# Where ninety products of an output projection stand beside a recurrence: one constant in a hybrid recurrent block

## The chip, the cores and the metric

The kernel runs on one core of one Trainium2 chip. The metric is the device time of one execution in microseconds (us), as the median of several runs. The engines are named as in the profile: PE (TensorE, with its weight loads PEld), DVE (VectorE), ACT (ScalarE), POOL (GpSimd) and SP (SyncE, which issues the transfers).

## What is computed

One layer of a diffusion backbone on 1024 latent tokens and a prefix of 256 context tokens, D = 1024, all in float32. Two token mixers read the same modulated input: an RG-LRU (width 1280, a linear recurrence over tokens in two directions) and an RWKV-7 (16 heads of 64, a matrix recurrence in two directions). Their outputs are merged and a SwiGLU follows.

```python
def wkv7_scan(r, w, k, v, a, b, S0):          # the second recurrence
    def step(S, inp):
        sa = jnp.einsum('dbhij,dbhj->dbhi', S, a_t)
        S = S * w_t[..., None, :] + sa[..., :, None] * b_t[..., None, :] + v_t[..., :, None] * k_t[..., None, :]
        y = jnp.einsum('dbhij,dbhj->dbhi', S, r_t)

def merge(lru, rwkv, g_lru, g_rwkv, p):
    m = sigmoid(g_lru) * (lru @ p['w_o_lru']) + sigmoid(g_rwkv) * (rwkv @ p['w_o_rwkv'])
    return m @ p['w_out']

x = x + g_m * merge(...)
x = x + g_f * swiglu(modulate(rms_norm(x)), w_ffn_in, w_ffn_out)
```

The change concerns `lru @ w_o_lru` (1024 tokens, 1280 inputs, 1024 outputs), "the products" below, and the steps of `wkv7_scan` beside which they run.

## The kernel before

A float32 product is made from three TensorE products of parts: each operand is split into a high part (`hi`) and a rest (`lo`), and hi·hi, hi·lo and lo·hi are accumulated. A 128x512 output tile of `lru @ w_o_lru` needs 10 blocks of inputs times 3, so 30 products; there are 2 halves of the tokens (q) times 8 blocks of outputs (o), 16 tiles, 480 products in all.

The program is written as phases. Input projection, the RG-LRU and the preparation of the RWKV operands come first. `phase_b` runs the RWKV recurrence in 40 steps of 32 tokens: steps 0 to 7 are the context, steps 8 to 39 the latents. The heads are in two halves a = 0, 1, each a generator (`wkv_chain`). One step of one half is, on PE, `ru<-tvu,skb` (16 products into PSUM tile `ru`), then a copy to `rs`, then `ru<-rs,xc` (16 products), four copies of 32 rows from `ru` into the state tile `tvu`, then `pn<-tvu,ska` and two copies into the next `tvu`, and for latent steps `py<-tvu,skb`, which gives the output rows `y`. The copies alternate between ACT and DVE (`copy`, L990). So a half is a chain PE, ACT or DVE, PE, ACT or DVE, PE; the other half and the products fill what lies between. Names carry the step and the half: `ru8_0` is step 8, half 0.

The products come from the generator `lru_out` (L1058 to L1098). For q it first makes ten split inputs: loads `lh` and `lu`, a GELU on `lu` (ACT), `lh*lu` (POOL), the high part `lhi` (ACT, L68) and the rest `llo` (POOL, L69); ten buffers each. Then for each o it loads `olr` (640 KB, a single buffer), makes `olh` (ACT, L68, two casts) and `oll` (POOL, L69, two subtractions), two buffers each, loads `olg` and takes its sigmoid (ACT), issues 30 products into PSUM tile `pol` (two buffers, L1092), multiplies on DVE (L1097) and stores `t1`. The tile of q = 0, o = 4 is `pol0_4`. The generator hands out one product at each call.

`phase_b` calls it in two ways. `FILL0` products are drawn before `wkv_setup`; the others are drawn inside the loop over steps, at two places of each step, in a count that grows with the step so that `480 - FILL0 - TAIL` are out at the end; `TAIL` (45) are left behind the loop. While a product is drawn inside the loop, `k.pe_after` ties it behind the last scan product on PE by an ordering edge.

What order the engines get is not the order of the code. The framework records all instructions with a priority (their place in the code) and then lists them, engine by engine, by simulating the program with a model of durations; buffers of a pool and the ordering edges limit it. Each engine executes its list in that order. So drawing a product earlier in the code gives it a better priority and fewer ties; where it ends up on each engine is decided by that listing.

Of the kernel before, what the change touches and what calls it, by code (L numbers as in the profile page):

```python
# [1097 lines left out]
            nc.sync.dma_start(k.t1_d[o * P:(o + 1) * P, sl], g)  # L1098


FILL0 = 0
LASTN = 2
CTXP = 8
CTXO = 0
# [18 lines left out]
def phase_b(k):  # L1123
    tc = k.tc
    k.gnp = k.root.enter_context(tc.tile_pool(name="gnp", bufs=1, side="right"))
    with tc.tile_pool(name="bp", bufs=1) as k.bp, tc.tile_pool(name="olp", bufs=1) as op, \
# [6 lines left out]
        done = 0  # L1133
        for _ in range(FILL0):
            next(fill)
# [6 lines left out]
        for s in range(NSTEP + 1):  # L1142
            for i, a in enumerate((0, 0, 1, 0, 1, 1, 0, 1)):
# [15 lines left out]
                if i in FILLAT:  # L1159
                    at = s + (FILLAT.index(i) + 1) / len(FILLAT)  # L1160
                    while done < (480 - FILL0 - TAIL) * (at + CTXW * min(at, 8)) / (NFEND + 8 * CTXW):
                        next(fill, None)
# [523 lines left out]
```

## Time and profile before

| | us |
|---|---|
| runs | 3083.84, 3095.47, 3108.86 (median 3095.47) |
| the profiled execution | 3079.55, span 3077.7 |
| PE busy | 2707.6 (88%) |
| DVE, ACT, POOL busy | 1890.6, 1456.4, 1012.4 |
| mean granted TensorE clock | 0.924 |
| the scan's latent steps, from the trace | about 1684 to 2093 |

The profiled execution lies 15.9 us under the median of the runs. Busy time is a union of the records of an engine; the profile cuts the span into 40 slices of 77 us each for the curves of busy tenths and granted clock.

### The profile page before, as it was taken

The page shows a single profiled execution, that of the slowest core. Times are in us where ns is not written, and L with a number is a line of the kernel's source. Part 1 is how long each engine was busy: PE and PEld are TensorE (multiplying, and loading weights), DVE is VectorE, ACT ScalarE, POOL GpSimd, SP SyncE. Part 2 cuts the span into 40 slices and gives each one's busy share as a digit, 9 for nine tenths or more (in the row PEclk, how much of TensorE's full clock was granted, in tenths as well). Part 3 has the DMA queues.
Part 4 walks back from the last instruction along what each step waited for, and adds up shares of the span by engine and source line. Part 5 has one row for each costly group of instructions (what it writes and reads, how often), then busy time and mean ns, then how long its engine had stood idle before and what let it go on. Part 6 is the DMA issues. An engine that isn't in the chain of part 4 may idle for free. (4 is left out here: it accounts for less than half of the span.)

```text
span 3077.7 us, 57133 instructions
## 1 busy us (share of the span) xinstructions
PE 2707.6 (88%) x22526; PEld 2159.6 (70%) x22526; DVE 1890.6 (61%) x2843; ACT 1456.4 (47%) x2647; POOL 1012.4 (33%) x896
## 2 busy tenths in 40 slices
PE   5988988889899878887889788777999999999998
PEld 4776766667677666676656666555788888888888
DVE  7588898994667977889872333564785323223234
ACT  3476777783467565767433343454334111111114
POOL 4344444452445555666333130235431000000000
PEclk9899999999999979988569998888999999999999
DMA  5333334322455456556766787988753111121112
GB/s 207 95 117 123 124 104 134 111 85 77 133 152 146 119 123 141 124 137 158 200 196 218 228 258 220 253 252 261 269 214 127 58 48 50 41 61 42 42 57 73
DMA packets 379602, 429.18 MB, mean 139 GB/s; under 512 B 134166, under 2 KB 286150, under 8 KB 371398
## 3 DMA queue, kind: packets, MB, share of 16 engines
q1 hardware_dynamic: 379334, 425.53, 47.4%
q8 instruction: 178, 2.92, 0.4%
q14 instruction: 90, 0.74, 0.1%
HBM read 286.87 MB, written 126.26 MB: 134 GB/s over the span
## 5 line engine op out<-in xcount | busy, mean ns | idle before, releaser
L88 PE MATMUL pin<-h1024hi,whi 128*128 128x512 f32 (+1 forms) x1024 | 430.5, 421 | 47.5 <-DVE whi L230 15.4
L90 PE MATMUL pin<-h1024hi,wlo 128*128 128x512 f32 (+1 forms) x1024 | 420.9, 414 | 10.7 <-POOL wlo L231 10.6
L89 PE MATMUL pin<-h1024lo,whi 128*128 128x512 f32 (+1 forms) x1024 | 425.8, 416 | 4.1 <-DVE h1024lo L120 4.1
L231 POOL TENSOR_TENSOR wlo<-wraw,whi 128x512 fp32r<-128x512 f32 (+1 forms) x144 | 211.7, 1471 | 306.6 <-DVE whi L230 167.8
L88 PEld LDWEIGHTS pin<-h1024hi,whi 128*128 128x128 f32 (+1 forms) x1024 | 203.3, 199 | 102.0 <-DVE whi L230 15.9
L90 PEld LDWEIGHTS pin<-h1024hi,wlo 128*128 128x128 f32 (+1 forms) x1024 | 201.5, 197 | 64.5 <-POOL wlo L231 17.7
L89 PEld LDWEIGHTS pin<-h1024lo,whi 128*128 128x128 f32 (+1 forms) x1024 | 203.4, 199 | 50.0 <-DVE h1024lo L120 6.6
L54 ACT ACT_TABLE_LOAD x164 | 210.4, 1283 | 18.3 <-DVE gd L499 5.9
L987 PE MATMUL pn<-tvu,ska 128*64 128x64 f32 (+1 forms) x2496 | 157.4, 250 | 36.1 <-ACT tvu L990 19.2
L1434 DVE TENSOR_TENSOR sil<-sil,pfu 128x512 f32<-128x512 f32 x44 | 30.3, 688 | 242.0 <-PE pfu L90 242.0
L388 DVE SCALAR_TENSOR_TENSOR lxc<-lup,c_lru_conv_w,lxc 120x512 f32<-120x512 f32 (+3 forms) x198 | 161.1, 837 | 15.9 <-ACT lxc L386 15.2
L987 PEld LDWEIGHTS pn<-tvu,ska 128*64 128x64 f32 (+1 forms) x2496 | 119.9, 156 | 71.8 <-ACT tvu L990 23.8
L1442 DVE SCALAR_TENSOR_TENSOR x<-pfo,modv,x 128x512 f32<-128x512 f32 (+1 forms) x112 | 74.2, 671 | 132.4 <-PE pfo L90 132.4
L990 ACT COPY tvu<-ru 32x256 f32<-32x256 f32 x193 | 70.1, 363 | 126.8 <-DVE tvu L990 77.8
L68 ACT CAST whi_fi<-wraw_fi 128x1024 fp32r<-128x1024 f32 x48 | 50.5, 1053 | 167.6 <-PE pfg L89 50.4
L724 DVE TENSOR_TENSOR it<-bp,X 128x62 f32<-128x62 f32 (+25 forms) x186 | 122.1, 657 | 3.9
L230 DVE CAST whi<-wraw 128x512 fp32r<-128x512 f32 (+1 forms) x144 | 76.3, 531 | 76.3 <-PE pin L89 36.6
L687 ACT COPY bc<-pm 32x256 f32<-32x256 f32 x160 | 98.8, 617 | 50.9 <-PE pm L683 48.4
L673 PE MATMUL pkt<-c_ident,kb 128*128 128x128 f32 x320 | 59.2, 315 | 65.6 <-DVE kb L657 41.5
L987 PE MATMUL ru<-tvu,skb 128*32 128x64 f32 (+1 forms) x2560 | 93.0, 243 | 26.8 <-ACT tvu L990 8.7
L725 DVE TENSOR_TENSOR X<-X,it 128x62 f32<-128x62 f32 (+25 forms) x186 | 113.7, 611 | 3.9
L432 POOL TENSOR_TENSOR lxc<-la 120x512 f32<-120x512 f32 (+3 forms) x66 | 86.8, 1318 | 80.1 <-ACT la L54 68.3
(374 smaller groups left out, 7512.9 us busy)
## 6 DMA issues: line engine op xcount, KB each, us to landing
skb<-skb_d SPq DMA_DIRECT2D x40, 1024.0 KB
wraw<-in_w_in_dram SPq DMA_DIRECT2D x142, 256.0 KB
wraw_fi<-in_w_ffn_in_dram SPq DMA_DIRECT2D x48, 512.0 KB
skb_d<-kr SPq DMA_DIRECT2D x160, 128.0 KB
ska_d<-kt SPq DMA_DIRECT2D x160, 128.0 KB
skb_d<-km SPq DMA_DIRECT2D x160, 128.0 KB
ska<-ska_d SPq DMA_DIRECT2D x40, 512.0 KB
wmr<-in_w_modT_dram SPq DMA_DIRECT2D x32, 512.0 KB
```

Source lines behind the costliest of these rows:

```text
L54: ins = self.nc.scalar.activation(*a, **b).ins
L88: nc.tensor.matmul(out, wh, xh, start=first, stop=False)
L89: nc.tensor.matmul(out, wh, xl, start=False, stop=False)
L90: nc.tensor.matmul(out, wl, xh, start=False, stop=last)
L230: nc.vector.tensor_copy(hi, raw)
L231: (nc.gpsimd if INLO else nc.vector).tensor_tensor(lo, raw, hi.bitcast(F32), ALU.subtract)
L388: nc.vector.scalar_tensor_tensor(xc, tap(j), k.lcw[r, t, d, j:j + 1], xc, ALU.mult, ALU.add)
L432: nc.gpsimd.tensor_tensor(xc, a, a, ALU.mult)
L687: nc.scalar.copy(bc[g, :, 4 * i:4 * i + 4].rearrange("s t e h -> s h e t"), pm[64 * c + 32:64 * c + 64, :, d, :, 32:64])
L724: nc.vector.tensor_tensor(tv, bpt[:, :, t + 1:32, t:t + 1].to_broadcast(sh), X[:, :, t:t + 1, 0:t + 1].to_broadcast(sh), ALU.mult)
L725: nc.vector.tensor_tensor(X[:, :, t + 1:32, 0:t + 1], X[:, :, t + 1:32, 0:t + 1], tv, ALU.add)
L987: k.pe_last = nc.tensor.matmul(*a, **b, start=True, stop=True).ins.name
```

## The change

One constant. `FILL0` is the number of products that are drawn from `lru_out` before the set-up of the scan, without a tie to a scan product; with 90 of them drawn there, the loop draws 345 instead of 435 over the same steps.

```diff
-FILL0 = 0
+FILL0 = 90
```

The code that reads it:

```python
        for _ in range(FILL0):
            next(fill)
        with tc.high_priority(offset=SETO):
            wkv_setup(k)
...
                    while done < (480 - FILL0 - TAIL) * (at + CTXW * min(at, 8)) / (NFEND + 8 * CTXW):
                        next(fill, None)
                        done += 1
```

What this does to the engines' lists is seen at three places. First PE, around the last products of `ru8_0` that read the first latent block `xc8` (step 8, half 0). Before:

```order
L1092 MATMUL pol0_4_16072<-lhi0_8_15083,olh0_4_16063 128x512
L987 MATMUL pn7_1_16238<-tvu1_1_14937,ska1_14925 64x64 x16
L987 MATMUL ru8_0_16218<-rs8_0_16235,xc8_15994 32x64 x10
L1092 MATMUL pol0_4_16072<-llo0_8_15084,olh0_4_16063 128x512
L1092 MATMUL pol0_4_16072<-lhi0_8_15083,oll0_4_16064 128x512
L1092 MATMUL pol0_4_16072<-lhi0_9_15093,olh0_4_16063 128x512
L1092 MATMUL pol0_4_16072<-llo0_9_15094,olh0_4_16063 128x512
L1092 MATMUL pol0_4_16072<-lhi0_9_15093,oll0_4_16064 128x512
L987 MATMUL ru8_1_16285<-tvu1_2_14938,skb2_14929 32x64 x2
```

And of the change, at the same scan products:

```order
L1092 MATMUL pol0_5_15813<-llo0_9_15021,olh0_5_15804 128x512
L1092 MATMUL pol0_5_15813<-lhi0_9_15020,oll0_5_15805 128x512
L987 MATMUL ru8_0_16306<-rs8_0_16323,xc8_16102 32x64 x12
L1092 MATMUL pol0_6_16097<-lhi0_0_14930,olh0_6_16088 128x512
L1092 MATMUL pol0_6_16097<-llo0_0_14931,olh0_6_16088 128x512
L987 MATMUL ru8_0_16306<-rs8_0_16323,xc8_16102 32x64
L987 MATMUL ru8_1_16372<-tvu1_2_15168,skb2_15159 32x64 x13
L1092 MATMUL pol0_6_16097<-lhi0_0_14930,oll0_6_16089 128x512
L1092 MATMUL pol0_6_16097<-lhi0_1_14940,olh0_6_16088 128x512
```

The tile `pol0_5` stands wholly ahead of the end of `ru8_0` and most of `pol0_6` ahead of `pn8_0`; before, both are spread over steps 8 to 15. Counted over the whole list, the products ahead of the first scan product of a step are 90 and 90 (before, and of the change) at step 7, 92 and 107 at step 8, 155 and 213 at step 9, 256 and 295 at step 19, 328 and 353 at step 28, 419 and 419 at step 38.

Second, PE in one round of a later step (step 20, half 0), before:

```order
L987 MATMUL ru20_0_18391<-rs20_0_18408,xc20_18153 32x64 x16
L1092 MATMUL pol1_0_18130<-lhi1_4_18065,oll1_0_18122 128x512
L1092 MATMUL pol1_0_18130<-lhi1_5_18075,olh1_0_18121 128x512
L1092 MATMUL pol1_0_18130<-llo1_5_18076,olh1_0_18121 128x512
L1092 MATMUL pol1_0_18130<-lhi1_5_18075,oll1_0_18122 128x512
L1092 MATMUL pol1_0_18130<-lhi1_6_18085,olh1_0_18121 128x512
L987 MATMUL py19_1_18476<-tvu1_1_14937,skb1_14928 32x64 x12
L987 MATMUL ru20_1_18500<-tvu1_2_14938,skb2_14929 32x64 x16
```

And of the change:

```order
L987 MATMUL ru20_0_18443<-rs20_0_18460,xc20_18207 32x64 x16
L1092 MATMUL pol1_1_18012<-llo1_7_17204,olh1_1_18003 128x512
L1092 MATMUL pol1_1_18012<-lhi1_7_17203,oll1_1_18004 128x512
L1092 MATMUL pol1_1_18012<-lhi1_8_17213,olh1_1_18003 128x512
L987 MATMUL py19_1_18526<-tvu1_1_15167,skb1_15158 32x64 x16
L987 MATMUL ru20_1_18550<-tvu1_2_15168,skb2_15159 32x64 x16
```

A round holds four or five products before and three or four with the change.

Third, ACT in step 8: `olh0_5`, `olh0_6` and so on are the casts of the projection's weights, `olg` its gates, `lu1`, `lhi1` the inputs of the second half of the tokens, and the L990 rows the copies of the scan. Before:

```order
L68 CAST olh0_5_16347<-olr0_5_16345 128x640 x2
L54 ACTIVATE olg0_5_16353<-olg0_5_16353 128x512
L990 COPY tvu0_2_14935<-ru8_0_16218 32x256 x3
L990 COPY tvu0_0_14933<-pn8_0_16304 64x512
L990 COPY tvu1_2_14938<-ru8_1_16285 32x256 x2
L68 CAST olh0_6_16879<-olr0_6_16877 128x640 x2
L990 COPY tvu1_2_14938<-ru8_1_16285 32x256
L990 COPY ys8_0_16398<-py8_0_16381 128x256
```

And of the change:

```order
L68 CAST olh0_5_15804<-olr0_5_15802 128x640 x2
L54 ACTIVATE olg0_5_15810<-olg0_5_15810 128x512
L68 CAST olh0_6_16088<-olr0_6_16086 128x640 x2
L54 ACTIVATE olg0_6_16094<-olg0_6_16094 128x512
L990 COPY tvu0_2_15165<-ru8_0_16306 32x256 x3
L68 CAST olh0_7_16435<-olr0_7_16433 128x640 x2
L54 ACTIVATE olg0_7_16441<-olg0_7_16441 128x512
L54 ACT_TABLE_LOAD
L54 ACTIVATE lu1_0_17128<-lu1_0_17128 128x512
L54 ACTIVATE lu1_1_17138<-lu1_1_17138 128x512
L990 COPY tvu0_0_15163<-pn8_0_16391 64x512
L990 COPY tvu1_2_15168<-ru8_1_16372 32x256 x2
```

The casts of `olh0_6` and `olh0_7`, the table load and the first two GELUs of the second half stand ahead of the copy from `pn8_0`; before, `olh0_7` and the GELUs stand in steps 11 and 12. A few rows further down in the list of the change, the cast of `olh1_0` and one more GELU stand ahead of the copy from `pn8_1`; before, it stands in step 14.

## Rows read from the trace of the kernel before

**Rows 1.** The profile's page: the span, and PE's busy tenths and granted clock in 40 slices
```profile
span 3077.7 us, 57133 instructions
...
PE   5988988889899878887889788777999999999998
...
PEclk9899999999999979988569998888999999999999
```
**Rows 2.** Busy time of each engine by stretch, then granted clock, DMA share, GB/s
```profile
core 0: us, PE busy (x) PEld busy (x) DVE busy (x) ACT busy (x) POOL busy (x), PEclk, DMA share, GB/s
1620.00:1684.00 64.00, 61.08 (x809) 43.50 (x811) 16.39 (x30) 20.14 (x41) 25.01 (x15) 0.97 0.73 231
1684.00:1912.00 228.00, 185.46 (x4995) 142.75 (x4990) 78.12 (x150) 88.99 (x200) 43.47 (x32) 0.92 0.80 234
1912.00:2093.00 181.00, 137.38 (x3111) 103.61 (x3099) 103.66 (x141) 86.05 (x225) 62.89 (x28) 0.86 0.84 241
2093.00:2170.00 77.00, 63.46 (x349) 48.00 (x350) 38.95 (x49) 38.48 (x79) 36.09 (x15) 0.84 0.87 271
```
**Rows 3.** PE in order of time, end of step 7 and step 8: start, us, instruction
```profile
1668.82 0.39 PE L1092 MATMUL pol<-lhi,olh 128*128 128x512 f32 x1
1669.05 0.40 PE L1092 MATMUL pol<-llo,olh 128*128 128x512 f32 x1
...
1671.81 0.39 PE L1092 MATMUL pol<-llo,olh 128*128 128x512 f32 x1
1672.13 0.31 PE L987 MATMUL ru<-rs,xc 32*32 32x64 f32 x8
...
1678.32 0.33 PE L987 MATMUL pn<-tvu,ska 128*64 128x64 f32 x2
```
**Rows 4.** The tile xc, issues of its loads: duration ns, first and last start
```profile
L975 SPq DMA_DIRECT2D xc<-x_d x8: 320/400/1146, 1624.6 to 1972.9; - x8
```
**Rows 5.** ACT in order of time, steps 7 to 9; in brackets idle before and releaser
```profile
1651.47 1.35 ACT L68 CAST olh<-olr 128x640 fp32r<-128x640 f32 x2 [1.12 <-DMA olr<-in_w_o_lru_dram]
...
1665.89 1.35 ACT L68 CAST olh<-olr 128x640 fp32r<-128x640 f32 x2 [9.80 <-DMA olr<-in_w_o_lru_dram]
...
1675.42 1.36 ACT L68 CAST olh<-olr 128x640 fp32r<-128x640 f32 x2 [5.30 <-DMA olr<-in_w_o_lru_dram]
...
1680.37 0.58 ACT L990 COPY tvu<-pn 64x512 f32<-64x512 f32 x1 [1.44 <-PE pn L987]
1681.22 0.75 ACT L990 COPY tvu<-ru 32x256 f32<-32x256 f32 x2 [0.27 <-PE ru L987]
1683.74 1.35 ACT L68 CAST olh<-olr 128x640 fp32r<-128x640 f32 x2 [1.77 <-DMA olr<-in_w_o_lru_dram]
...
1688.06 0.56 ACT L990 COPY tvu<-pn 64x512 f32<-64x512 f32 x1
```
**Rows 6.** ACT, then PE, in order of time at steps 12 and 13
```profile
1724.99 0.63 ACT L54 ACTIVATE olg<-olg 128x512 f32<-128x512 f32 x1 [5.01 <-DMA olg<-gl_d]
1725.62 1.28 ACT L54 ACT_TABLE_LOAD   x1
1726.92 1.15 ACT L54 ACTIVATE lu<-lu 128x512 f32<-128x512 f32 x2
...
1728.51 1.12 PE L987 MATMUL pn<-tvu,ska 128*64 128x64 f32 x16 [5.67 <-ACT tvu L990]
...
1732.93 0.63 PE L1092 MATMUL pol<-llo,olh 128*128 128x512 f32 x1
1733.35 0.63 PE L1092 MATMUL pol<-lhi,oll 128*128 128x512 f32 x1
```
**Rows 7.** What PE waited for, 1684 to 2093: total us, times, longest
```profile
PE pn L987 <- ACT tvu L990: 16.9, 10, 5.7
PE ru L987 <- issue: 16.7, 12, 2.4
PE py L987 <- issue: 14.5, 8, 3.7
```

## The prediction

> **What bounds the kernel now.** I read the page first, then the busy time by stretch, then PE and ACT in order of time. On the page PE is the busiest engine and its granted clock is ragged in the middle of the span [rows 1]. The change touches the scan there, so the stretches count. From 1620 to 1684 us (the end of the context steps and latent step 8) PE is busy for 61.1 of 64 us at a granted clock of 0.97: PE itself is the bound, and the products that stand between the scan's matmuls delay the scan one for one. From 1684 to 2093 (steps 9 to 39) PE is busy for 185.5 of 228 and 137.4 of 181 us, at 0.92 and 0.86 [rows 2]: 86 us of PE are idle, and a step is a chain PE, copy, PE, copy. After 2093 come the 45 products of the tail, behind the scan in PE's list, and the merge, which needs the last outputs of the scan, so I let a delay of the scan's end reach the end of the kernel in full.
>
> Two things are to be seen in the rows. Products follow each other on PE at 0.23 us at full clock (1668.82 to 1669.05 [rows 3]) and at 0.42 us at half clock (1732.93 to 1733.35 [rows 6]). And the first matmuls of step 8 that need `xc8` run at 1672.13 (some just before) [rows 3], although that load was issued at 1624.6 [rows 4], more than 40 us earlier. So PE does not wait for it. The simulated listing must see a long wait there, since it packs products in front of these matmuls; on the chip there is none.
>
> **The change part by part.** First, the ninety products themselves: in both lists 90 stand ahead of step 7, nearly the same ones at the same places. Taking the tie away moves nothing there: 0 us. No instruction is added or removed; every load, cast and store of the projection exists as before.
>
> Second, step 8. Ahead of step 9 stand 213 products instead of 155: 58 more. PE has 2.9 us idle in that stretch [rows 2], so they are paid: 58 x 0.23 = 13.3 us. The lower bound would be 0 if the wait for `xc8` were real; the rows say it is not, so I take 13.3.
>
> Third, their weights. ACT executes in order, and the casts of `olh` wait for loads. A load into the single buffer `olr` starts when POOL has finished with the tile before; the casts run at 1651.47, 1665.89, 1675.42 and 1683.74, each after an idle wait for the load [rows 5], that is rounds of 14.4, 9.5 and 8.3 us. With the change the casts of `olh0_6` and `olh0_7`, a gate (0.63), a table load (1.28) and two GELUs (1.15) stand ahead of the copy from `pn8_0`. Two rounds after 1675.42 at 8.3 to 9.5 us are 1692.1 to 1694.5; with the cast (1.36) and the rest this is 1696.5 to 1698.9 for a copy that ran at 1680.37 [rows 5, 6]: 16.1 to 18.5 us late, 2.8 to 5.2 us more than the products alone make it. I take 4.0. Behind that copy stands `pn8_0`'s successor `ru9_0` on PE, and then the whole chain. The cast of `olh1_0` one round later, ahead of the copy from `pn8_1` (1688.06 [rows 5]), gives about the same. SP's queue moves too: the loads of `olr` and the stores of `t1` come earlier between the same scan loads, and the DMA engines are busy for 0.73 of the stretch, less than later [rows 2]; I put 0 on it.
>
> Fourth, a stall that goes. At step 12 ACT waits 5.01 us for the gate's load, then does the table load and the two GELUs, and PE stands idle for 5.67 us behind it [rows 6]. That group now lies in step 8 and is in the third term: -5.7 us. If something else takes its place there, 0.
>
> Fifth, what steps 9 to 38 get back. They lose the 58 products, 33 before step 28 and 25 after. At the granted clocks of 0.92 and 0.86 a share of 16% and 28% of the time is at half clock, so a product is worth 0.26 and 0.28 us: 33 x 0.26 + 25 x 0.28 = 15.6 us if PE were the bound in every round. If every round ended on a copy or another wait, it would be 0. There are 60 rounds (30 steps, two halves), each one product shorter, and the three largest causes alone make 30 waits of PE in them [rows 7]. A round that already waits only waits longer. So I take half: -7.8 us.
>
> Sum: 13.3 + 4.0 - 5.7 - 7.8 = +3.8 us. On the profiled execution's 3079.55 this is 3083.4; that execution lies 15.9 us under the median of the runs, and the prediction is for a median: 3095.47 + 3.8, or 3099.
>
> **The rivals.** *The scan thins out and the clock falls.* In the rows the granted clock falls with PE's density: 0.97 at 95% busy, 0.92 at 81%, 0.86 at 76% [rows 2]. The change takes about one product in five out of every round. If the stretch at 0.92 falls to 0.86 and the one at 0.86 to 0.80, the share at half clock grows by 12% of the time, 27 + 22 = 49 us; PE is busy for 79% of it and does half the work, so 49 x 0.79 / 2 = 19 us are lost: 3.8 + 19 = +23, or 3118. Against it: PE loses about 0.5 us of work (two products) in a step of 13.6 (409 us over 30 steps). The Trainium skill, "TensorE: Matmul & The Clock Gate", section "HAM oscillation — how this bites in real kernels", says that gaps in matmul work bring the half clock back, again and again in a loop with waits. The trace agrees so far as its ragged clock goes; by that rule the change would cost these 23 us instead of 4.
>
> *The free gap.* The step 8 wait is real, or PE reaches it with time to spare, and the 58 products fill it: 0 + 4.0 - 5.7 - 7.8 = -9.5, or with everything given back -17: 3078 to 3086. For it speaks only that the listing put them there; against it the load of `xc8` [rows 4] and the full PE [rows 2].
>
> *ACT's queue is the bound in step 8 (the slower side).* Place: the casts of `olh0_6`, `olh0_7` and `olh1_0` ahead of the scan's copies. If each round of load, cast and subtraction takes the 14.4 us that one of them took [rows 5], the third comes at 1718.6, the copy from `pn8_1` at 1721 instead of 1688.06: 33 us late, 19.6 beyond the products, so +19.4 in all: 3115. It is slower by over 1% (31 us) from rounds of about 18 us. For it: all four casts of [rows 5] waited for their load, and the copies of the ten inputs of the second half also move from steps 12 to 17 up into steps 8 to 12. Against it: the two rounds at that very place took 9.5 and 8.3.
>
> **How the numbers follow.** The forecast with its own range, from all given back and no ACT term (13.3 - 5.7 - 15.6 = -8) to nothing given back and the upper ACT term (13.3 + 5.2 - 5.7 = +13), is 3087 to 3108: chance 0.56. The clock 0.15, the free gap 0.12, ACT's queue 0.13, anything else 0.04. The runs of the kernel before lie 11.6 us under and 13.4 us over their median, and a median of new runs can lie several us off as well. So the range is 3082 to 3125: it takes in the clock and ACT's queue at their prices and most of the free gap. About 1% (31 us) is what a measurement of this kernel can tell from no change. Faster by that needs the free gap, all given back and more: 0.03. Slower by that needs the clock or ACT's queue at more than the prices above, or both: 0.12. Within 1%: 0.85.
>
> **What would show it.** Right: PE stays above 90% busy through step 8, the first `ru<-rs,xc` of step 9 comes 13 to 19 us later than before against the end of step 7, ACT's row `olh<-olr` waits for the load two or three times in that stretch with an L990 copy directly behind, no idle PE of 5 us at step 12, and steps 9 to 38 shorter by about 14 us in sum (a quarter us each, and the stall). Wrong, second step: step 9 begins no later. Wrong, third: the copy from `pn8_0` runs right behind its matmuls. Wrong, fifth: steps 9 to 38 as long as before (then +11), with PE waiting more on copies; or longer, with a granted clock under 0.90 from 1700 on, which is the clock's case. If the mean clock and the length of the context steps change, the first step was wrong.

## The result, and the profile after

The change makes the kernel slower: 3105.76 us (3098.09 to 3114.50) beside 3083.85 us (3073.88 to 3108.86) for the kernel before on the same chip, a ratio of 1.0067 (95% interval 1.0055 to 1.0079), so +20.7 us by the ratio. A second measurement gave 1.0081 (1.0061 to 1.0100). That is within 1%, and 3105.76 lies in the range, but the forecast was a step of +3.8 us, so about 17 us were not foreseen. The rest of this text looks for them.

From the page of the change, the lines that answer to [rows 1]: span, and PE's busy tenths and granted clock in 40 slices.
```profile
span 3099.1 us, 57147 instructions
...
PE   5888888889899878896889888678899999999998
...
PEclk9999999899999879997568898868999999999999
```
Busy time of each engine by stretch (columns as in [rows 2]), cut at the same work as there: up to the end of step 7 and most of step 8, the rest of step 8, steps 9 to 28, 28 to 39.
```profile
1620.00:1684.00 64.00, 62.37 (x553) 42.77 (x552) 11.99 (x21) 17.37 (x34) 23.09 (x14) 0.83 0.62 206
1684.00:1705.00 21.00, 20.73 (x206) 15.16 (x208) 3.94 (x7) 5.92 (x10) 7.10 (x6) 1.00 0.48 145
1705.00:1933.00 228.00, 188.35 (x5173) 145.47 (x5168) 81.29 (x154) 88.54 (x202) 41.33 (x31) 0.90 0.82 241
1933.00:2114.00 181.00, 128.81 (x2967) 96.66 (x2966) 97.52 (x141) 85.09 (x223) 57.47 (x27) 0.79 0.83 230
```
PE is full up to step 9, as it was, but for 64 us it runs at 0.83 of the clock in place of 0.97 [rows 2], and behind step 28 the clock is 0.79 in place of 0.86.

A finer cut follows the scan itself. Each step has one copy of `ru` into `rs` for half 0; the time from that copy in one step to that in another is how long the scan took. The same view, cut at these copies of steps 6, 9, 28 and 39, of the kernel before:
```profile
1627.88:1683.86 55.98, 53.50 (x719) 38.54 (x721) 14.45 (x26) 18.37 (x37) 23.74 (x14) 1.00 0.78 250
1683.86:1912.89 229.03, 186.49 (x5039) 143.69 (x5041) 78.67 (x150) 89.13 (x200) 43.47 (x32) 0.92 0.80 234
1912.89:2081.49 168.60, 126.73 (x2910) 95.67 (x2908) 96.69 (x134) 80.40 (x206) 57.84 (x27) 0.87 0.86 247
```
and of the change:
```profile
1625.19:1708.93 83.74, 81.71 (x773) 57.38 (x773) 15.94 (x29) 24.96 (x46) 32.81 (x21) 0.88 0.58 191
1708.93:1927.08 218.15, 182.29 (x5004) 140.93 (x5005) 78.17 (x149) 84.86 (x194) 37.44 (x28) 0.90 0.82 241
1927.08:2107.17 180.09, 125.41 (x2900) 94.44 (x2898) 95.35 (x136) 79.82 (x206) 56.78 (x26) 0.78 0.83 233
```
Steps 6 to 9 cost 28 us more, steps 9 to 28 give back 11, steps 28 to 39 cost 11.5 more. Both kernels were profiled once more (e5, e6), and here are all kernels by this cut, in us; the columns of products count those ahead of the first scan matmul of step 9 and of step 28 in PE's list, "not 90" means that 90 products have no tie, and each time of a stretch is from one profile.

| kernel | products 9 / 28 | tied | steps 6–9 | 9–28 | 28–39 | ratio (95%) |
|---|---|---|---|---|---|---|
| before | 155 / 328 | all | 56.0, 60.4 | 229.0, 230.5 | 168.6, 167.0 | |
| change | 213 / 349 | not 90 | 83.7, 84.5 | 218.2, 225.5 | 180.1, 178.9 | 1.0067, 1.0081 |
| e1 | 213 / 349 | all | 72.7 | 238.8 | 177.7 | 1.0082 (1.0063–1.0101) |
| e2 | 156 / 328 | not 90 | 71.2 | 218.3 | 170.3 | 1.0038 (1.0023–1.0052) |
| e3 | 153 / 289 | all | 59.3 | 232.1 | 155.0 | 1.0005 (0.9990–1.0020) |
| e4 | 215 / 388 | not 90 | 80.8 | 229.0 | 163.2 | 1.0082 (1.0062–1.0102) |
| e7 grouped | 155 / 328 | all | 45.7 | 225.0 | 162.7 | 0.9876 (0.9856–0.9897) |
| e8 grouped | 213 / 349 | not 90 | 72.4 | 229.6 | 189.4 | 1.0015 (0.9996–1.0034) |
| e9 | 213 / 349 | not 90 | 85.9 | 217.0 | 188.9 | 1.0114 (1.0096–1.0133) |
| e10 | 120 / 349 | not 90 | 45.3 | 240.5 | 180.2 | 1.0006 (0.9990–1.0022) |
| e11 grouped | 133 / 319 | all | 47.4 | 222.7 | 189.2 | 0.9935 (0.9913–0.9957) |
| e12 grouped | 155 / 328 | not 90 | 50.2 | 231.2 | 168.8 | 0.9924 (0.9899–0.9949) |

With two profiles each, the difference of the means is +25.9 for steps 6 to 9, -7.9 for 9 to 28, +11.7 for 28 to 39, and -4.0 and -4.5 for what lies ahead and behind: +21.2, which is what was measured. What lies ahead differs as much within one kernel (the copy of step 6 comes at 1627.9 and 1637.5 us before, at 1625.2 and 1632.2 in the change). What lies behind does not: it takes 996.2 and 997.0 us before, 991.9 and 992.3 in the change. So a part of the loss of steps 28 to 39 comes back behind the scan, and from step 28 to the end the change costs 7.2 us.

**What is new in step 7.** PE in order of time in the change, at the start of step 7 (start, us, instruction):
```profile
1643.10 0.29 PE L987 MATMUL ru<-rs,xc 32*32 32x64 f32 x2
1643.32 0.30 PE L987 MATMUL ru<-tvu,skb 128*32 128x64 f32 x2
1643.55 0.29 PE L987 MATMUL ru<-rs,xc 32*32 32x64 f32 x2
...
1647.18 0.29 PE L987 MATMUL ru<-rs,xc 32*32 32x64 f32 x2
1647.40 0.42 PE L987 MATMUL ru<-tvu,skb 128*32 128x64 f32 x14
```
and the same matmuls in the kernel before:
```profile
1645.79 0.52 PE L987 MATMUL ru<-rs,xc 32*32 32x64 f32 x20
1646.24 0.65 PE L987 MATMUL ru<-tvu,skb 128*32 128x64 f32 x32
```
Each matmul of PE's list shows as two records here (26 of the list, 52 records). Before, the two groups run one behind the other: 52 records in 1.1 us. In the change PE's list has one matmul of each group by turns (x2 in the rows), and from turn to turn PE needs 0.23 us: 4.7 us for the same 52. PE is "busy" all the time, so no view of waits shows it. A second block of such turns, `ru` of step 7 with `ru` of step 8, lies at 1673.5 to 1676.4; the kernel before has none there either. From the first scan matmul of step 6 to that of step 9 the lists have 71 changes from one group to another before, 96 in the change (e10 below counts steps 6 and 7 alone, in another way). The Trainium skill, "TensorEngine Tiling (Array Packing)", section "Key Properties", says that a change of the tiling mode drains TensorE; the trace fits that, with 0.23 us for a turn of two records in place of 0.02 us a record, but it does not show that the drain is what takes the time.

Right behind it the clock falls. The change in stretches of 10 us through step 7, where the last but two column is the granted clock:
```profile
1640.00:1650.00 10.00, 9.79 (x117) 6.76 (x119) 1.27 (x3) 1.45 (x4) 4.64 (x2) 0.94 0.72 277
1650.00:1660.00 10.00, 9.03 (x66) 5.90 (x62) 1.38 (x2) 4.99 (x8) 3.03 (x2) 0.50 0.32 67
1660.00:1670.00 10.00, 10.00 (x44) 7.15 (x44) 1.80 (x3) 0.00 (x0) 0.00 (x0) 0.71 0.54 190
```
The stretch from 1650 is wholly at the lower of the two levels (1.2 GHz) with PE busy for 9.0 of 10 us; the fall comes at 1648.8. Ahead of it PE did the turns of `ru` with `ru`; the turns of `ru` with `pn`, which the kernel before has too, follow at 1651.7 and run at the lower level. The first profile of the kernel before stays at 1.00 there.

### The profile page after: what moved, and what is told of

The parts are those of the page before. It is cut to its first block, busy times and chain, and to the rows that moved or that the text cites. A ratio compares the mean times of both kernels' runs of the same rounds, so it can differ in the third digit from the quotient of the medians.

```text
span 3099.1 us, 57147 instructions
## 1 busy us (share of the span) xinstructions
PE 2718.6 (88%) x22526; PEld 2164.8 (70%) x22526; DVE 1899.9 (61%) x2843; ACT 1456.9 (47%) x2647; POOL 1006.3 (32%) x896
## 5 line engine op out<-in xcount | busy, mean ns | idle before, releaser
L88 PE MATMUL pin<-h1024hi,whi 128*128 128x512 f32 (+1 forms) x1024 | 428.2, 418 | 49.6 <-DVE whi L230 14.8
L990 ACT COPY tvu<-ru 32x256 f32<-32x256 f32 x193 | 69.9, 362 | 174.1 <-DVE tvu L990 111.1
L987 PE MATMUL ru<-tvu,skb 128*32 128x64 f32 (+1 forms) x2560 | 100.8, 248 | 34.5 <-DVE tvu L990 17.1
L69 POOL TENSOR_TENSOR oll<-olr,olh 128x640 fp32r<-128x640 f32 x32 | 51.3, 1623 | 216.8 <-ACT olh L68 131.3
```

What stands on the lines that cost most here:

```text
L88: nc.tensor.matmul(out, wh, xh, start=first, stop=False)
L987: k.pe_last = nc.tensor.matmul(*a, **b, start=True, stop=True).ins.name
```

## The experiments

**e1 and e2: tie or count?** The change does two things at once. e1 keeps every product tied but draws as many ahead of step 9 as the change; e2 unties 90 but draws as many as the kernel before.
```diff
-CTXW = 1
+CTXW = 2.565
```
```diff
-FILL0 = 0
+FILL0 = 90
-CTXW = 1
+CTXW = -0.241
```


> All products stay tied to the steps (FILL0 = 0), but they are drawn at another pace (CTXW = 2.565 in place of 1), so that 213 of them stand ahead of step 9 as in the change, and 349 ahead of step 28 as in the change. Theory A, the count ahead of step 9 sets the loss, not the tie: the time is that of the change, 1.005 to 1.008 of the kernel before (+15 to +25 us), the first result copy of step 9 comes about 80 to 84 us after that of step 6 (before 56.0, change 83.7). Theory B, the loss comes from products without a tie, which may be put in other places of the set-up: the time is that of the kernel before within 5 us, and the distance from step 6 to step 9 is 56 us plus 13 for the 58 products.

> 90 products without a tie as in the change (FILL0 = 90), but the rest is drawn so that 156 stand ahead of step 9 and 328 ahead of step 28, as in the kernel before (CTXW = -0.241). Theory A (count): within 4 us of the kernel before, step 6 to step 9 about 56 us. Theory B (no tie): 15 to 25 us slower, as the change.

Steps 6 to 9, of e1 and then of e2 (columns as in [rows 2]):
```profile
1629.74:1702.46 72.72, 69.41 (x773) 49.91 (x773) 15.94 (x28) 25.07 (x46) 32.80 (x21) 1.00 0.69 224
```
```profile
1626.31:1697.46 71.15, 69.81 (x719) 48.63 (x721) 14.55 (x26) 20.33 (x40) 26.77 (x16) 0.86 0.60 197
```
Both theories are half right. Against the mean of before (58.2) the count alone costs 14.5 us, at full clock (16.7 against the 56.0 of the profile that is at full clock too); the missing tie alone costs 13.0, with as many matmuls as before but PE busy for 69.8 us and the clock at 0.86. Together 27.5; the change shows 25.9. In e2 the `ru` matmuls of step 7 alternate as in the change (1644.42 to 1649.41); in e1 they do so for three turns only. The whole time of e1 is that of the change (+25 us), although it lost less in these steps: its steps 9 to 28 took 238.8 us at a clock of 0.87. e2 is 11.7 us slower than before.

**e3 and e4: the thinner steps alone, the early cost alone.**
```diff
-while done < (480 - FILL0 - TAIL) * (at + CTXW * min(at, 8)) / (NFEND + 8 * CTXW):
+while done < 145 * min(at, 8) / 8 + 7.1875 * max(at - 8, 0):
```
```diff
-FILL0 = 0
+FILL0 = 90
-while done < (480 - FILL0 - TAIL) * (at + CTXW * min(at, 8)) / (NFEND + 8 * CTXW):
+while done < 115 * min(at, 8) / 8 + 9.0625 * max(at - 8, 0):
```


> All tied; up to step 8 drawn as in the kernel before, and from step 8 at the pace of the change (7.19 a step in place of 9.06), so that 58 products more are left for the stretch behind the scan. This is the thinning of steps 9 to 39 without the cost at step 8; the 58 products at the end cost about 58 x 0.23 = 13 us there. Theory of the forecast (a product taken out of a round gives back half of its time): steps 9 to 39 shorter by 8 us, in all +5 us. Theory of the clock (the thinner steps run at half clock more): granted clock from step 9 to step 39 lower by 0.02 to 0.06, these steps not shorter or up to 19 us longer, in all +13 to +32 us. What the trace of the change shows (steps 9 to 28 shorter by 5 without its stall, steps 28 to 39 longer by 11.5): in all about +20 us.

> 90 products without a tie and 213 to 215 ahead of step 9 as in the change, but from there the pace of the kernel before (9.06 a step), so that the products run out with the scan and none is left behind it. This is the cost at step 8 without the thinning; the stretch behind the scan loses 45 products, 45 x 0.23 = 10 us. Theory that the loss is made at step 8 alone (step 6 to step 9 longer by 27.7 us in the change): steps 9 to 39 as long as before (about 398 us), in all +28 - 3 - 10 = about +15 us. Theory that half of it comes from the thinned steps 28 to 39 (+11.5 us in the change): these steps keep the 168.6 us of before. Theory that the stretch behind the scan is not bound by the products: in all +25 us.

e3, steps 9 to 28 and 28 to 39:
```profile
1694.62:1926.74 232.12, 194.08 (x5003) 147.22 (x5004) 78.42 (x150) 88.25 (x201) 40.32 (x30) 0.89 0.78 231
1926.74:2081.69 154.95, 124.84 (x2951) 92.88 (x2951) 90.27 (x131) 79.74 (x203) 51.45 (x24) 0.87 0.91 260
```
With the pace of the change, steps 9 to 39 take 387 us, 10.5 less than before. All of it lies in steps 28 to 39, which are the shortest of all the kernels, at a clock of 0.87; so thinner steps need not make that stretch longer or lower its clock. In steps 9 to 28 they gave nothing back: with 37 products fewer than before these take 2.3 us more than the mean, the clock is 0.89 in place of 0.92 and 0.93, and PE is busy for 194.1 us in place of 186.5. There the clock theory has its fall of the clock. The sum is near the forecast's -7.8, but it is a single profile, of the slowest run of this kernel (3091.13, median 3080.37). The stretch behind the scan grew by 11 us for 60 products (105 in the list in place of 45), and in all there is nothing to speak of (+1.5 us). e4 has the early cost in full (80.8 us), and its steps 28 to 39 are even shorter than before; but the 45 products taken from behind the scan saved nothing there (998.0 us beside 996.6), so that it is as slow as the change. The theory that these products bound that stretch was wrong on this side.

**e5 and e6: the same two kernels again.**

> The change once more, to see which of its stretches come again. In its first profile: PE's two kinds of ru matmuls of step 7 alternate for 4.3 us, half clock follows for 17.1 us, step 6 to step 9 takes 83.7 us; steps 9 to 28 take 218.2, steps 28 to 39 180.1 with 32.9 us for step 33 to 34. Theory A (the loss is in the order on PE in step 7 and in the count): alternation and half clock come again in step 7, step 6 to step 9 again 80 to 85 us. Theory B (half clock falls where chance puts it): step 6 to 9 comes out anywhere between 70 and 84. The stall of step 34 comes again if it belongs to the change (28 to 33 us), and is 11 to 20 us if it is chance. Time 1.005 to 1.009 of the kernel before.

> The kernel before once more, for the spread of its stretches from one execution to the next. In its first profile: step 6 to step 9 56.0 us, steps 9 to 28 229.0, steps 28 to 39 168.6, from there to the end 996.2. If single stretches carry the difference between the kernels, they come out within 3 us; if the granted clock moves them about, within 10.

In the change the alternation, the half clock in step 7 and the stall of steps 33 to 34 all came again (32.9 and 33.8 us; before 12.1 and 12.5). The kernel before had 13.7 us of half clock in step 7 this time and none the first time, and its steps 6 to 9 took 4.4 us more: the half clock alone is partly chance, the alternation is not. Among the tied kernels without grouping (before, e6, e1, e3) that place shows half clock twice in four profiles; in those without the tie (change, e5, e2, e4, and e9 below) in all five, for 13.7 to 20.5 us. That is too few to say that the turns cause it.

**e7 and e8: groups kept whole.** An order without a wait ties the first scan matmul of a group behind the last of the group before, which takes the changes between groups from 688 to 301 in all.
```diff
-    def mm(*a, **b):
-        k.pe_last = nc.tensor.matmul(*a, **b, start=True, stop=True).ins.name
+    def mm(*a, first=False, **b):
+        ins = nc.tensor.matmul(*a, **b, start=True, stop=True).ins
+        if first and getattr(k, "pe_last", None) is not None:
+            k.tc.add_manual_dep(ins, k.pe_last, NOSYNC, reason="group")
+        k.pe_last = ins.name
```
(`first` is true for the first matmul of each of the four groups.)

> The kernel before with the scan's matmuls of one group (ru of the state, ru of the input, pn, py) kept in one piece on PE, by an order without a wait from the last matmul of a group to the first of the next: 301 changes between groups in place of 688. Theory A (matmuls of different shapes in alternation cost 0.23 us a pair, in groups 0.02 each; the trace of before has about 27 to 41 us of such pairs in steps 0 to 6, 11 in steps 6 to 9, 28 in steps 9 to 28, 27 in steps 28 to 39, half of it hidden by copies): 30 to 60 us faster, steps 0 to 6 shorter by 15 to 30 of 160.7. Theory B (the alternation fills time in which PE would wait for copies anyway): within 6 us of the kernel before. Rival on the other side (a group that waits now holds up the next group, which was ready): 10 to 30 us slower, with PE idle ahead of ru and pn.

> The change (90 products without a tie) with the same order of groups as the run beside it, so that step 7 has no alternation; ahead of step 9 stand 213 products, in the grouped kernel before 155. Theory A (of the change's 27.7 us between steps 6 and 9 some 11 come from alternation and the half clock behind it, 17 from 58 products and ACT's queue): against the grouped kernel before 12 to 18 us more between steps 6 and 9 and no half clock in step 7, in all 5 to 15 us slower than that kernel. Theory B (the whole loss is the count): 20 to 28 us slower than the grouped kernel before.

The grouped kernel before takes 3047.60 us, 1.24% less than the kernel before: it beats both. Steps 0 to 6 are shorter by 13 us (148.8; less than the 15 to 30 expected), steps 6 to 9 by 12.5, steps 9 to 39 by 10. For the grouped change both theories were too low: it is 43 us slower than the grouped kernel before. In the profiles it loses 26.7 in steps 6 to 9, though nothing alternates, and as much again in steps 28 to 39, of which 11.5 come back behind the scan. Of the 26.7 in steps 6 to 9, 20.1 are busy time of PE (60.7 us beside 40.6; 58 products are 13.3 at full clock, and the clock is 0.91 beside 0.96), and 6.6 are idle time (11.7 beside 5.1). The idle time goes back to ACT's list (e8, ACT in order of time; in brackets idle before and releaser):
```profile
1667.70 1.35 ACT L68 CAST olh<-olr 128x640 fp32r<-128x640 f32 x2 [6.20 <-DMA olr<-in_w_o_lru_dram]
...
1676.45 1.36 ACT L68 CAST olh<-olr 128x640 fp32r<-128x640 f32 x2 [6.87 <-DMA olr<-in_w_o_lru_dram]
...
1683.89 0.36 ACT L993 COPY tvu<-ru 32x256 f32<-32x256 f32 x1
```
Between 1661.5 and 1683.89 no copy of the scan stands on ACT, only casts that wait for their weights, two gates, a table load and two GELUs. So with the alternation gone, ACT's queue does hold up the scan there, as the third rival had it, but for the smaller part of the loss.

**e9: the stall at step 33.** In the change DVE, in order of time behind step 32:
```profile
1997.27 0.43 DVE L990 COPY tvu<-ru 32x256 f32<-32x256 f32 x1 [0.43 <-ACT tvu L990]
2007.50 1.23 DVE L1245 TENSOR_TENSOR gy<-gy,gy 128x1024 f32<-128x1024 f32 x1 [9.79 <-DMA gy<-y_d]
```
The add of the group norm waits for its load (which reads rows that the scan has just stored), and the scan's copies stand behind it; PE waits with them (view of waits, 1995 to 2040):
```profile
PE ru L987 <- DVE tvu L990: 10.2, 1, 10.2
```
e9 holds this add back behind the last scan copy and starts that norm a step later.
```diff
-GNS = (28, 32, 36)
+GNS = (28, 33, 36)
...
+        if k.turn % 5 in COPYD:
+            k.dve_last = ins.name
...
-    nc.vector.tensor_tensor(y, y, y1, ALU.add)
+    ins = nc.vector.tensor_tensor(y, y, y1, ALU.add).ins
+    if tb == 2:
+        k.tc.add_manual_dep(ins, k.dve_last, NOSYNC, reason="late")
```


> The change, but the group norm's add of token block 2 (gy2, line L1245) can only stand on DVE behind the scan's copies of step 33: its generator starts one step later and an order without a wait holds the add behind the last scan copy on DVE. In the change it stands ahead of the copies of pn32_1 and ru33_0, and DVE waits 9.8 us there for the load; in the kernel before it stands ahead of a copy of step 34 and waits 4.6. Ahead of step 32 all lists are those of the change. Theory A (this place makes the loss of steps 28 to 39, 179.5 us on average in two profiles of the change against 167.8): no wait of more than 5 us there, step 33 to 34 12 to 18 us in place of 33, steps 28 to 39 168 to 173, in all 5 to 12 us faster than the change (1.004 to 1.006 of the kernel before). Theory B (the thinner steps at half clock make it): steps 28 to 39 stay at 177 to 182 and the time stays at 1.007 to 1.008.

The add no longer waits and step 33 to 34 takes 9.6 us; but the next step stalls in its place (35.9 us), now on ACT:
```profile
2043.07 1.28 ACT L54 ACT_TABLE_LOAD   x1 [19.31 <-DMA olg<-gl_d]
```
A gate of the products waits 19 us for its load, the scan's copies behind it. Steps 28 to 39 take 188.9 us, and the kernel is slower than the change. Theory A named a real stall, and taking it away alone gains nothing.

**e10: the change with groups in steps 6 and 7 alone** (the edit of e7 without `py`, and in these two steps only).
```diff
+GRP = (6, 7)
...
-            mm(t[gr, 0, v], skb[seen, unit(d, i), 32:64], tvu[seen, d, i])
+            mm(t[gr, 0, v], skb[seen, unit(d, i), 32:64], tvu[seen, d, i], first=v + g == 0 and s in GRP)
```

> The change with the scan's matmuls of steps 6 and 7 alone kept in groups: 14 changes between groups in these two steps in place of 80 (kernel before: 48). The products between them move by up to one step; 220 stand ahead of step 10 in place of 221. So steps 6 to 10 are compared: kernel before 69.3 us, change 95.2. Theory A (what the tie brought, about 13 us, is the alternation in steps 6 and 7 and the half clock behind it): 80 to 86 us for steps 6 to 10 and 8 to 15 us faster than the change in all, 1.002 to 1.005 of the kernel before. Theory B (half clock comes anyway and ACT's queue takes what is freed, as in the grouped change, 72.4 us for steps 6 to 9): 92 to 98 us, within 4 us of the change.

Steps 6 to 10, the products in them being those of the change but moved by up to a step:
```profile
1621.74:1702.87 81.13, 73.53 (x1092) 54.43 (x1092) 20.97 (x38) 30.14 (x58) 34.91 (x22) 0.96 0.77 240
```
81.1 us in place of 95.3 and 96.4, and the time is that of the kernel before (+1.8 us). Theory A holds for the steps; in all, the gain is larger than its 8 to 15 us. The profile is of the fastest run of this kernel (3074.65, median 3086.27); beside the mean of the change's two it has 14.7 us less in steps 6 to 10, 7.0 less ahead of them, 5.4 less from there to step 28 and 7.0 less behind the scan. It does not part what the tie brought from the turns that the kernel before has in these steps too: grouping took 12.5 us out of them there as well (e7).

**e11: fewer products ahead of step 9, grouped** (e7 with another pace).
```diff
-CTXW = 1
+CTXW = 0.5
```

> The grouped kernel before with fewer products ahead of step 9: 133 in place of 155 (CTXW = 0.5), the 22 others in the steps from 9 on. Theory A (each product ahead of step 9 costs 0.23 us and comes back only in part): steps 6 to 9 shorter by 3 to 5 us than the grouped kernel before (45.7), in all 1 to 5 us faster than it, 0.986 to 0.987 of the kernel before. Theory B (there the products fill gaps already, the denser steps from 9 on pay): 2 to 8 us slower than the grouped kernel before, 0.988 to 0.990.

Neither: steps 6 to 9 are no shorter (47.4), and the kernel is some 18 us slower than e7: steps 28 to 39, with 107 products in place of 98, take 189.2 us in place of 162.7, and the stretch behind is 11.5 us shorter.

**e12: e7 without the tie, the count as before** (e8 with another pace).
```diff
-CTXW = 1
+CTXW = -0.241
```

> 90 products without a tie and 155 ahead of step 9 (CTXW = -0.241), with the scan's matmuls in groups. Its lists up to step 28 are those of the grouped kernel before but for a handful of neighbours in step 7; behind step 28 the group norm's add of token block 2 (gy2) stands on DVE ahead of the copies of pn32_1 and ru33_0, as in the change, in place of a place behind ru33_0 (grouped kernel before, where it waited for nothing). Theory A1 (the missing tie costs nothing but through the alternation it brings): steps 6 to 9 within 5 us of the 45.7 of the grouped kernel before. Theory B1 (products without a tie cost in another way): 10 to 15 us more in these steps. Theory A2 (the place of the add makes the stall of steps 33 and 34): DVE waits 8 to 12 us there, step 33 to 34 25 to 34 us in place of 8.4, steps 28 to 39 170 to 180 in place of 162.7, the time 0.990 to 0.994 of the kernel before in place of 0.9876. Theory B2 (the place doesn't matter, the thinner steps made the stall): no wait over 5 us there, steps 28 to 39 160 to 166, 0.986 to 0.989.

Steps 6 to 9 take 50.2 us: A1, the missing tie costs 4.5 us once nothing alternates, with a clock of 0.93 beside 0.96. A2 fell: the add stands where it stands in the change and waits for nothing, since its load has landed by then (idle ahead of it 0.03 us). Its whole time is still 0.9924. In steps 9 to 28 ACT and DVE have the same lists as in e7, and PE's differ by the place of one product, and yet (e7, then e12):
```profile
1661.53:1886.55 225.02, 177.29 (x5057) 139.06 (x5049) 78.74 (x150) 89.22 (x200) 43.51 (x32) 0.92 0.82 242
```
```profile
1666.01:1897.17 231.16, 182.77 (x5057) 143.30 (x5048) 78.73 (x150) 89.43 (x200) 43.56 (x32) 0.88 0.80 234
```
the same matmuls took 6 us more at 0.88 than at 0.92. A single profile of this stretch is good to about that much.

## Why the prediction was right or wrong

**First step, "taking the tie away moves nothing there: 0 us": wrong.** Up to step 7 the products do stand where they stood, and the forecast looked no further. But the listing also turned the scan's own matmuls of steps 6 to 8 from groups into turns. That, and the half clock which came with it in all five profiles, cost 13.0 us in steps 6 to 9 with the count as before (e2), and 11.7 us in the whole time. How much of it is turns and how much is clock no run parts. With the groups kept whole, 4.5 us of it are left (e12 beside e7). The prediction gave the sign of this itself: the context steps' length changed, with step 6 to 7 at 22.8 and 23.5 us in place of 19.1. It is not the whole miss, though: e1 has every tie, and ends as late as the change.

**Second and third term, 13.3 + 4.0 = 17.3 for 58 products and ACT's queue: the sum about right, the third term not seen.** Beside the profile of before that is at full clock too, e1 shows 16.7 us; of these, 15.9 are more busy time of PE (69.4 beside 53.5 us) and only 0.8 more idle time. So the 58 products were paid on PE, at somewhat more than 0.23 us each, and no wait of 4 us stands beside them. ACT's rows in the change came as described (weights waited for, a copy behind; they answer to [rows 5]):
```profile
1671.85 1.35 ACT L68 CAST olh<-olr 128x640 fp32r<-128x640 f32 x2 [16.50 <-DMA olr<-in_w_o_lru_dram]
1681.99 1.35 ACT L68 CAST olh<-olr 128x640 fp32r<-128x640 f32 x2 [3.91 <-DMA olr<-in_w_o_lru_dram]
...
1694.25 1.35 ACT L68 CAST olh<-olr 128x640 fp32r<-128x640 f32 x2 [10.37 <-DMA olr<-in_w_o_lru_dram]
...
1702.05 1.35 ACT L68 CAST olh<-olr 128x640 fp32r<-128x640 f32 x2 [4.29 <-DMA olr<-in_w_o_lru_dram]
...
1706.42 0.58 ACT L990 COPY tvu<-pn 64x512 f32<-64x512 f32 x1
```
The copy from `pn8_0` stands at 1706.42, behind the last of them, a gate, the table load and two GELUs. But its matmuls had ended only at 1704.9 (the row of 30 records at 1703.78, 1.15 us long), since the products stand in front of them, and PE then waits 0.42 us: the copy was late by 1.5 us. Behind a first round of 20.3 us the rounds were 10.1, 12.3 and 7.8 us, not the 14.4 of the slower rival. Only where PE is not full (e8) does ACT's queue add time.

**Fourth term, the stall at step 12 goes, -5.7: right that it goes.** PE's waits in the change, steps 9 to 28:
```profile
PE pn L987 <- ACT tvu L990: 3.6, 3, 1.9
```
No wait of 5 us is left; the kernel before has 14.8 us of this kind there, the 5.67 of [rows 6] among them. What that alone was worth no run shows.

**Fifth term, -7.8 from thinner steps: not borne out.** The text ahead of the prediction has 353 products ahead of step 28 in the change; that is the count ahead of its second half, and ahead of its first scan matmul there are 349. (The 256 and 295 at step 19 are likewise the counts at step 20.) So 37 products leave steps 9 to 28 and 21 the rest, which leaves the -7.8 as it is. In the change, steps 9 to 28 are 7.9 us shorter, the stall included; e2 has as many products there as the kernel before and is 11.5 us shorter, and e3, thinned alone, is 2.3 us longer. So no gain from the thinning is to be seen there. Steps 28 to 39 are 11.7 us longer in the change, where a gain of 2.9 was forecast; e3 is 12.9 us shorter there. The sign of the prediction for this step came: steps 9 to 39 are not shorter but 3.7 us longer, with a clock of 0.90 and below.

What makes steps 28 to 39 longer is open. The pace of the products alone does not fix it: e3 has 79 products in these steps and takes 155.0 us, e11 has 107 and takes 189. But of the seven profiles with 76 to 79 products the other six take 178 to 189 us, and the six with 92 to 98 take 163 to 170, so the pace can have a part in it. The length goes with the time for which DVE waits for the loads of the group norm's adds: 19.1 and 17.4 us before, 27.2 and 27.8 in the change, 12.9 in e3, 30.9 in e8, 23.8 in e11 (the idle time of DVE directly ahead of these adds, summed; over the 14 profiles its correlation with the length of these steps is 0.84). That is no proof of a cause. Which add or gate comes too early depends on the whole list; e9 and e12 show that no single place makes it.

The prediction also let a delay of the scan's end reach the end of the kernel in full. It did not: over the 12 profiles with 45 products behind the scan, the longer steps 28 to 39 are, the shorter is the stretch behind (correlation -0.71), and in the change it is 4.5 us shorter.

**The rivals.** The clock did fall, from 0.92 and 0.93 to 0.90 and 0.89 in steps 9 to 28 and from 0.87 and 0.85 to 0.78 and 0.80 behind, and the total came within 3 us of that rival's +23. That rival is not refuted. In steps 9 to 28 all six profiles with the pace of the change (136 products) have a clock of 0.87 to 0.90, and five of the six with 172 or 173 have 0.92 or 0.93 (e12 has 0.88); the length does not follow, with 226.3 us beside 226.7 on average in the kernels without grouping throughout (e10, which has 226 products there, left out). It looks as if the lower clock took what the thinning would have given back, but no run shows that by itself. Behind step 28, e3 kept 0.87, so there thinner steps are not enough for a lower clock. In the change PE is idle for 55 and 56 us of steps 28 to 39 in place of 42 and 39, behind stalled copies, and the lower clock comes with that. The free gap did not exist: e1 paid for its 58 products. The Trainium skill, "TensorE: Matmul & The Clock Gate", section "HAM oscillation — how this bites in real kernels", puts the half clock down to gaps between matmuls; behind step 28 the trace agrees, in step 7 it comes with PE busy for 9.0 of 10 us.

By stretch, the means of two profiles beside the forecast are: steps 6 to 9, +25.9 beside 17.3; steps 9 to 28, -7.9 beside -5.7 - 4.8; steps 28 to 39, +11.7 beside -2.9; ahead and behind, -8.5 beside 0. So the point was low by the first step, which it had set to nothing, and most of all by the thinner steps, which gave nothing back and were followed by a loss behind step 28. That the time itself, 3105.76, came within 7 us of the forecast's 3099 is luck: the three runs that it started from had a median of 3095.47, 11.6 us above the 3083.85 of twenty.

## What to carry to other kernels

When an edit only moves filler work, compare the order of everything else on that engine too: a listing may turn the critical path's own matmuls from groups into turns, which here cost four times their length (4.7 us in place of 1.1) and shows up as busy time, not as a wait. Where small matmuls of different tile shapes are both ready, tie them group by group; here that was worth 1.24%, more than any placement of the products. And treat each transfer-dependent instruction that a listing puts ahead of a critical copy (a weight cast, a gate, an add) as a possible stall of the whole chain: removing one may only hand the wait to the next.

## What the hardware showed that was not expected

Turns of two records between the tiles 32*32 and 128*32 take 0.23 us each, where a run of one kind takes about 0.02 us a record (32 in 0.65 us). TensorE went to the lower level of its clock for 13.7 to 20.5 us in step 7 while PE was busy for over 90% of that time by the profile, in all five profiles in which a block of turns of `ru` with `ru` stands in front of that of `ru` with `pn`, and in two of the four with at most three turns in front of it. The four kernels with all groups kept whole have 3.4 to 6.9 us of half clock around step 7, so turns are not its only condition. And taking 45 products out of the stretch behind the scan did not shorten it (998.0 beside 996.6 us), while adding 60 made it 11 us longer.
